# Half-array matmuls of a hybrid attention and state space trunk, run on the whole array

## Chip, cores and metric

One core of a Trainium2 chip runs the whole program; the other cores are idle. The metric is the device time of one execution in microseconds, as the median of several runs, without what the host does.

## What is computed

Two layers of a trunk on 512 tokens of width 1024. Each layer normalises and modulates its input, mixes tokens in three branches (differential attention, latent attention, a gated state space branch), merges them through gates, and ends with a gated feed-forward block with a short convolution. The parts that the change touches, cut down:

```
# differential attention: 4 heads, two maps m of 64 features each
s = einsum('bhqmd,bhkmd->mbhqk', q, k) * 64**-0.5 + bias, causal
p = softmax(s);  out = einsum('bhqk,bhkv->bhqv', p[0] - lam * p[1], v)
# latent attention: 8 heads, 96 features for scores, 64 for values
p = softmax(einsum('bhqd,bhkd->bhqk', q, k) * 96**-0.5, causal)
out = einsum('bhqk,bhkd->bhqd', p, v)
# state space: 16 heads, chunks of 128 tokens
cs = cumsum(dt * a);  decay = exp(cs[l] - cs[s]), causal within a chunk
```

Inputs, weights and result are fp32.

## The kernel before

Tokens or features lie on the 128 partitions, and nearly all work is products on TensorE. Most of them take operands split in a high and a low part, both in the faster fp32r format: `mm3` (L141 to L143) issues high times high, high times low and low times high into one PSUM bank. Weights come by DMA in pieces of 512 KB, ScalarE makes the high part (L132), VectorE the low part (L133). `feat_groups` (512 tokens as moving columns) and `tok_groups` (L220 to L222, 256 columns) yield after every few products, so that they can be laid between others. Some products are plain fp32, which the trace records twice each.

A planner orders all engines' work by its own estimates, and picks the engine where the code says `nc.any`. In the two attentions TensorE's order is written out by hand instead (`manual_schedule`): `run` issues a unit's scores, some filling products (`fill`, from the gates, branches and next projections), an earlier unit's transposes, more filling, and the weighted values of one still earlier.

PSUM has two pools: "mb" for the large products, "ab" for the rest, five banks in the attentions.

- State space branch (`mix`, a group of four heads at a time). `decays` leaves the sums of the steps' logarithms in `cs_r`, 48 rows: 16 heads' high parts in rows 0 to 15, their low parts in rows 32 to 47. For each head a product of `sel`'s column with `cs_r` (L953) spreads one head's row over 128 partitions; VectorE makes `dec` from it (L955).
- Latent attention. Units are a head and a tile of 128 queries; heads are taken in pairs whose values lie side by side in `vv`, 64 columns each. `mla_unit`'s scores are an `mm3` on 96 rows, its softmax ends at L1156, `weights_T` transposes the probabilities (L1136), and `values` (L1168) multiplies 64 columns of `vv` by them. The two heads of a pair write the two halves of one bank, which is copied to `o_feat` when both are done (L1171). The scores run two units ahead of the transposes and three ahead of the values.
- Differential attention. `da_transpose` leaves for each map a tile of queries (high parts in the map's own 64 rows, low parts in the other 64) and one of keys (high parts in both), so that one product on 128 rows gives high times high and low times high (L1292). Queries' high parts times keys' low parts are a second product on the map's own 64 rows (L1293), with the keys' low parts of both maps in one tile `kl`. A unit has two such pairs of products, one for each map, with max(256, 128 (t + 1)) columns for the tile t of queries.

Of the kernel before, what the change touches and what calls it, by code (L numbers as in the profile page):

```python
# [9 lines left out]
F32 = mybir.dt.float32  # L10
# [8 lines left out]
P = 128  # L19
S = 512  # L20
# [45 lines left out]
def trunk_kernel(ctx: ExitStack, tc: tile.TileContext, a: dict, out: bass.AP):  # L66
# [26 lines left out]
    # ---------------------------------------------------------------- constants  # L93
# [9 lines left out]
    sel = cst.tile([48, SSM_H], F32R, name="sel")  # L103
    nc.vector.tensor_copy(out=sel[0:32], in_=ident[0:32, 0:SSM_H])
# [8 lines left out]
    # ---------------------------------------------------------------- weights  # L113
# [42 lines left out]
    def feat_groups(w, cols, nk, rhs, evac):  # L156
        """Two tiles of 128 output features; w is [nk*128, n], cols their first columns.
        A group is a function that fetches weights and one that yields after some products."""
        st = {}
        joined = cols[1] == cols[0] + P  # L160

        def group(k0):
            n = min(4, nk - k0)

            def prep():
                rows = w[k0 * P:(k0 + n) * P, :].rearrange("(k p) c -> p k c", p=P)
                if joined:
                    raw = load([(0, (n, 256), rows[:, :, cols[0]:cols[0] + 256])])
                    view = "p (k i c) -> p i k c"
                else:  # L170
                    raw = load([(i * n * P, (n, P), rows[:, :, c:c + P]) for i, c in enumerate(cols)])
                    view = "p (i k c) -> p i k c"
                wh, wl = split(raw, n * 256)
                bg(2)
                return [x[:, 0:n * 256].rearrange(view, k=n, i=2) for x in (wh, wl)]

            def mm(weights):
                vh, vl = weights
                if k0 == 0:
                    st["banks"] = [mbank(), mbank()]  # L180
                for k in range(n):
                    xh, xl = rhs(k0 + k)
                    for i in range(2):
                        mm3(st["banks"][i], vh[:, i, k], vl[:, i, k], xh, xl, k0 + k == 0, k0 + k == nk - 1)
                    if k0 + k == nk - 1:
                        for i in range(2):
                            evac(i, st["banks"][i])
                    yield 1.28
            return prep, mm
        return [group(k0) for k0 in range(0, nk, 4)]  # L190

    def tok_groups(w, segs, hh, hl, evac):
        """Up to 256 output columns, tokens on partitions."""
# [37 lines left out]
    def feat_halves(w, cols, nk, rhs, evac, joint, pool=None, spare=0):  # L231
        """As feat_groups, the tokens' first half before the second. With joint, evac gets whole rows.
        The weights of the last groups, spare in number, go to a pool of their own."""
# [35 lines left out]
    def latent_product(l, pool, hh, hl):  # L269
        """Tokens' latent queries, latent keys and values, rotary key and step sizes, a half of the tokens after the other.  # L270
        The weights of the last group go to a pool of their own."""
# [43 lines left out]
    def seam(last, norm, first, us):  # L315
        """The last two products before a norm and the first one after it, in halves of the tokens."""
# [41 lines left out]
    # ---------------------------------------------------------------- small vectors of a layer  # L358
# [3 lines left out]
    def mod_vectors(l, vp):  # L362
        """Bias of the modulation, the norms' gains, the state space branch's taps."""
# [69 lines left out]
    # ---------------------------------------------------------------- rotary tables  # L433
# [31 lines left out]
    # ---------------------------------------------------------------- conditioning  # L465
# [25 lines left out]
    # ---------------------------------------------------------------- modulation  # L491
    mod = [cst.tile([P, 48], F32, name=f"mod{l}") for l in range(DEPTH)]

    def mod_steps(l, j, pool=None):
        """Steps that together give 512 columns of a layer's modulation."""
# [46 lines left out]
    def mod_steps_pe(l, j, pool):  # L542
        """The same with products on the tensor engine."""
# [20 lines left out]
    def mod_queue(l, chunks):  # L564
        """Steps of several chunks; a chunk's sums over partitions come within the next chunk."""
        out, late = [], None
        for j in chunks:
            todo = mod_steps(l, j)
            out += todo[0:4] + ([late] if late else []) + todo[4:-1]
            late = todo[-1]  # L570
        return out + [late]

    # ---------------------------------------------------------------- relative bias, in blocks of causal tiles
# [10 lines left out]
    def rel_tables(bp):  # L584
        """Key positions, queries' positions less the buckets' starts, block-diagonal table of steps."""
# [8 lines left out]
        # differences of neighbouring buckets; halves of them, and of the ends' sum, for steps of -1 and 1  # L594
# [40 lines left out]
    def rel_bias(bp, tables, t, g):  # L635
        """Bias of 32 queries of a tile for all heads; a column of four queries needs the keys up to them only."""
# [31 lines left out]
    # ---------------------------------------------------------------- modulated norm  # L668
    def norm_r(np_, x_tok):
        """A token's reciprocal root mean square, on all partitions; after a step for each tile of tokens."""  # L670
# [33 lines left out]
    def norm_halves(np_, x, l, v_norm, sh0, sc0):  # L704
        """The norm of tiles whose last four come in halves of the tokens, as steps for seam()."""
# [35 lines left out]
    # ---------------------------------------------------------------- token mixing  # L741
    def mix(l, x, hh, hl, ckr, cq, latp, scope):
        """Gated sum of the branches, twice over."""
# [49 lines left out]
        # ---- latents of the latent attention  # L793
# [47 lines left out]
        cs_r = ssd.tile([48, S], F32R, name="cs_r")  # L841
        nc.vector.tensor_copy(out=cs_r, in_=zeros[0:48])
        cs, ncs, tot, ecs, te = (ssd.tile([P, T, SSM_H], F32, name=nm) for nm in ("cs", "ncs", "tot", "ecs", "te"))

        def decays():
            """Sums of the steps' logarithms within chunks, and what follows from them."""
# [17 lines left out]
        # ---- state space branch, a group of four heads at a time  # L864
        ys = []
        with ssd_scope:
            tails = []
            for g in range(SSM_G):
# [81 lines left out]
                for r in range(4):  # L950
                    h = 4 * g + r
                    lp_ = abank()
                    nc.tensor.matmul(lp_, sel[:, h:h + 1].broadcast_to([48, P]), cs_r, start=True, stop=True)  # L953
# [47 lines left out]
        with ExitStack() as att:  # L1001
# [6 lines left out]
            def feed(groups):  # L1008
                """Queues products that fill the gaps; the weights of the first two are fetched at once."""
                todo.extend(groups)  # L1010
                while len(ahead) < min(2, len(todo)):
                    ahead.append(todo[len(ahead)][0]())
# [11 lines left out]
            def fill(us=None):  # L1024
                """Filling products for about that many microseconds, or all that is queued."""
                owed[0] = owed[0] + us if us else 1e9
                while owed[0] > 0.6:
                    cost = next(filling)
                    owed[0] = owed[0] - cost if cost else 0.0
# [14 lines left out]
            # ---- latent attention, two heads at a time  # L1044
            def rope(x, n, cc, ss_, o):
                """x, o: [P, n.., 32]; cc, ss_ tables of the same shape"""
# [94 lines left out]
            def mla_unit(pr, h, t):  # L1141
# [20 lines left out]
                def values():  # L1162
                    if t == 0 and h == 0:
                        pairs[pr]["o"] = abank()
                    po, vv = pairs[pr]["o"], pairs[pr]["v"]
                    own = slice(h * MLA_V, (h + 1) * MLA_V)
                    for j in range(t + 1):
                        nc.tensor.matmul(po[own, t * P:n], vv[:, j, own], st["pT"][:, j * P:(j + 1) * P],  # L1168
                                         start=j == 0, stop=j == t)
                    if t == T - 1 and h == 1:  # L1170
                        nc.any.tensor_copy(out=o_feat[pr], in_=po)  # L1171
                return scores, turn, values

            def run(units, events, amounts, lag, later={}):
                """Scores of a unit, transposes of an earlier one, weighted values of one still earlier."""
# [51 lines left out]
            # ---- differential attention  # L1227
            ya = []
            heads = [{} for _ in range(DA_H)]

# [23 lines left out]
            def da_transpose(h, i):  # L1254
                """Queries' high parts over low parts, keys' high parts twice, keys' low parts; a tile for each map."""
# [7 lines left out]
                maps = (slice(0, DA_D), slice(DA_D, P))  # L1263
                if i == 1:
                    heads[h]["kl"] = kl = dap.tile([P, S], F32R, name="kl")
                for m, own in enumerate(maps):
# [3 lines left out]
                    lo = o[other] if i == 0 else kl[own]  # L1270
# [5 lines left out]
            def da_unit(h, t):  # L1276
# [3 lines left out]
                def scores():  # L1280
# [6 lines left out]
                    for m in range(2):  # L1287
                        mr = slice(m * DA_D, (m + 1) * DA_D)
# [4 lines left out]
                        nc.tensor.matmul(s_ps[:, 0:w], qT[mr], hd["kl"][mr, 0:w], start=False, stop=True)  # L1293
# [70 lines left out]
    def out_products(l, mo, m_, extra):  # L1364
        """Output projection and residual: the residual, the products of one half, those of the other."""
# [24 lines left out]
    # ---------------------------------------------------------------- gated conv feed-forward  # L1390
    class Ffn:
        """Blocks of features go through the up projection, the conv, the gate and the down projection."""
# [27 lines left out]
        def run(self, fp, extra):  # L1420
            """All but the last two products, which are returned."""
# [28 lines left out]
    # ---------------------------------------------------------------- the end  # L1450
    def finish(last, x):
        """The last product in halves of the tokens, whose rows go out as they come."""
# [30 lines left out]
    # ---------------------------------------------------------------- the trunk  # L1483
# [93 lines left out]
```

## Time and profile before

| | |
|---|---|
| median of 3 runs | 2136.69 us (2134.92 to 2140.43) |
| span of the profiled execution | 2134.3 us |
| TensorE products busy | 2109.5 us, 99% |
| TensorE weight loads busy | 1785.0 us, 84% |
| VectorE busy | 1416.2 us, 66% |
| ScalarE busy | 918.8 us, 43% |
| granted TensorE clock, mean | 0.999 |

The profile is of one execution. Its span runs from the first instruction to the last; the page gives no other time of that execution, and the median of the runs lies 2.4 us above the span. A product's end is modelled and overlaps the next one's start, so for TensorE the distance between starts tells the pace. "PE" is a product, "PEld" the load of its stationary operand; "128*64 128x128" is 128 rows by 64 columns of the array and a moving operand of 128 rows and 128 columns. An fp32 product stands as two records.

### The profile page before, as it was taken

Reading aid. Unit: us, or ns where it says so; the run is one execution under the profiler, and the core shown is the slowest. Engines: PE = TensorE matmul, PEld = TensorE weight load, DVE = VectorE, ACT = ScalarE, POOL = GpSimd, SP = SyncE. Lnnn points to the kernel's source line nnn. Section 1 sums busy time; section 2 is a strip of 40 time slices with the busy share of each in tenths; the row PEclk is TensorE's granted clock in tenths of the full one; section 3 lists DMA queues with packets and bytes.
Section 4 is the critical chain, followed back from the end, with each engine's and each line's share of the span. In section 5 each row is a group of like instructions: output and inputs, shape, how many; then the busy total and the mean of one; then the engine's idle time right before and its main releaser. Section 6 shows DMA issues by size and latency. Waiting matters only on the chain.

```text
span 2134.3 us, 30137 instructions
## 1 busy us (share of the span) xinstructions
PE 2109.5 (99%) x11469; PEld 1785.0 (84%) x11469; DVE 1416.2 (66%) x2730; ACT 918.8 (43%) x1689; POOL 137.5 (6%) x162
## 2 busy tenths in 40 slices
PE   7999999999999999999999999999999999999999
PEld 7888887788878988888898888878897888888888
DVE  7888877646766678658767787764566456553563
ACT  6644445434443354223344444454444334432441
POOL 4200011001100000000000000110110000000000
PEclk9999999999999999999999999999999999999999
DMA  7522242233444355555433222112232233323322
GB/s 264 148 75 79 65 131 81 71 112 98 149 137 148 113 179 169 190 177 164 154 128 95 64 70 82 56 47 73 86 88 83 87 129 99 96 93 98 99 87 82
DMA packets 224541, 237.19 MB, mean 111 GB/s; under 512 B 16126, under 2 KB 195742, under 8 KB 224142
## 3 DMA queue, kind: packets, MB, share of 16 engines
q1 hardware_dynamic: 221646, 232.63, 35.0%
q0 software_dynamic: 2752, 2.65, 0.5%
q8 instruction: 90, 1.47, 0.3%
q14 instruction: 53, 0.43, 0.1%
HBM read 226.30 MB, written 8.91 MB: 110 GB/s over the span
## 4 chain that ended last, share of the span: by engine, by line
PE 85%; DVE 5%; issue 5%; DMA 2%; POOL 1%; ACT 0%; SPq 0%; POOLq 0%; DVEq 0%; ACTq 0%
PE mb L141 20%; PE mb L142 20%; PE mb L143 20%; PE mb L220 3%; PE mb L222 3%; PE mb L221 3%; PE ab L1168 2%; PE ab L1136 1%; PE ab L1293 1%; DVE macc L518 1%; DMA wg<-in_ada_w_dram 1%; PE ab L961 1%; PE ab L1315 1%; PE ab L1292 1%; DVE wl L133 1%
## 5 line engine op out<-in xcount | busy, mean ns | idle before, releaser
L141 PE MATMUL mb<-hh,wh 128*128 128x512 f32 (+1 forms) x1376 | 541.2, 394 | 1.8 <-DVE modsum L530 0.9
L142 PE MATMUL mb<-hl,wh 128*128 128x512 f32 (+1 forms) x1376 | 533.0, 387 | 0.0
L143 PE MATMUL mb<-hh,wl 128*128 128x512 f32 (+1 forms) x1376 | 532.6, 387 | 0.0
L133 DVE TENSOR_TENSOR wl<-wr,wh 128x1024 fp32r<-128x1024 f32 (+2 forms) x312 | 374.9, 1203 | 211.9 <-ACT wh L132 209.5
L132 ACT ACTIVATE wh<-wr 128x1024 fp32r<-128x1024 f32 (+2 forms) x312 | 324.4, 1041 | 353.2 <-PE mb L142 270.8
L141 PEld LDWEIGHTS mb<-hh,wh 128*128 128x128 f32 x1376 | 258.4, 188 | 58.7 <-issue 6.4
L143 PEld LDWEIGHTS mb<-hh,wl 128*128 128x128 f32 x1376 | 258.6, 188 | 51.0
L142 PEld LDWEIGHTS mb<-hl,wh 128*128 128x128 f32 x1376 | 258.9, 188 | 50.0 <-issue 2.0
L1412 DVE SCALAR_TENSOR_TENSOR fu<-mb,vec,fu 128x510 f32<-128x510 f32 (+1 forms) x176 | 129.9, 746 | 92.0 <-ACT fu L1410 90.5
L220 PE MATMUL mb<-wh,hh 128*128 128x256 f32 x640 | 183.8, 287 | 0.0
L221 PE MATMUL mb<-wl,hh 128*128 128x256 f32 x640 | 181.0, 283 | 0.0
L222 PE MATMUL mb<-wh,hl 128*128 128x256 f32 x640 | 181.0, 283 | 0.0
L141 PE MATMUL mb<-gh,wh 128*128 128x512 f32 (+1 forms) x432 | 152.2, 352 | 0.0
L143 PE MATMUL mb<-gh,wl 128*128 128x512 f32 (+1 forms) x432 | 151.5, 351 | 0.0
L142 PE MATMUL mb<-gl,wh 128*128 128x512 f32 (+1 forms) x432 | 151.5, 351 | 0.0
L1410 ACT ACTIVATE fu<-mb,vec 128x512 f32<-128x512 f32 x88 | 67.7, 772 | 149.7 <-PE mb L143 149.7
L220 PEld LDWEIGHTS mb<-wh,hh 128*128 128x128 f32 x640 | 122.5, 191 | 3.1 <-issue 0.7
L221 PEld LDWEIGHTS mb<-wl,hh 128*128 128x128 f32 x640 | 122.6, 192 | 0.4
L222 PEld LDWEIGHTS mb<-wh,hl 128*128 128x128 f32 x640 | 122.6, 192 | 0.0
L518 DVE SCALAR_TENSOR_TENSOR macc<-wg,c_act,macc 128x512 f32<-128x512 f32 x140 | 104.8, 748 | 19.9 <-DMA wg<-in_ada_w_dram 19.1
L141 PE MATMUL mb<-yh,wh 128*128 128x512 f32 x256 | 105.8, 413 | 0.0
L142 PE MATMUL mb<-yl,wh 128*128 128x512 f32 x256 | 101.1, 395 | 0.0
(333 smaller groups left out, 3416.3 us busy)
## 6 DMA issues: line engine op xcount, KB each, us to landing
wr<-in_w_in_dram SPq DMA_DIRECT2D x88, 512.0 KB
wr<-in_ffn_w_up_dram SPq DMA_DIRECT2D x88, 512.0 KB
wg<-in_ada_w_dram SPq DMA_DIRECT2D x160, 256.0 KB
wr<-in_ffn_w_down_dram SPq DMA_DIRECT2D x40, 512.0 KB
wr<-in_w_in_dram SPq DMA_DIRECT2D x64, 256.0 KB
wm<-in_ada_w_dram SPq DMA_DIRECT2D x16, 512.0 KB
wr<-in_w_branch_c_dram SPq DMA_DIRECT2D x16, 512.0 KB
wr<-in_w_out_dram SPq DMA_DIRECT2D x16, 512.0 KB
```

The costliest lines, as they stand in the source:

```text
L132: nc.scalar.activation(hi[:, sl], raw[:, sl], AF.Copy)
L133: nc.vector.tensor_tensor(out=lo[:, sl], in0=raw[:, sl], in1=hi[:, sl], op=ALU.subtract)
L141: nc.tensor.matmul(o, lh, rh, start=first, stop=False)
L142: nc.tensor.matmul(o, lh, rl, start=False, stop=False)
L143: nc.tensor.matmul(o, ll, rh, start=False, stop=last)
L220: nc.tensor.matmul(o, hh[:, kk, ts_], wh[:, sl], start=first and k == 0, stop=False)
L221: nc.tensor.matmul(o, hh[:, kk, ts_], wl[:, sl], start=False, stop=False)
L222: nc.tensor.matmul(o, hl[:, kk, ts_], wh[:, sl], start=False, stop=last and k == 3)
L518: ins = nc.vector.scalar_tensor_tensor(out=acc[0], in0=rk, scalar=c_act[:, kk:kk + 1], in1=acc[0], op0=ALU.mult, op1=ALU.add)
L1168: nc.tensor.matmul(po[own, t * P:n], vv[:, j, own], st["pT"][:, j * P:(j + 1) * P], start=j == 0, stop=j == t)
L1410: nc.scalar.activation(u, bank, AF.Identity, bias=v[:, V_FCB + ti:V_FCB + ti + 1], scale=tap(2))
L1412: nc.vector.scalar_tensor_tensor(out=u[:, s_:], in0=bank[:, 0:S - s_], scalar=tap(2 - s_), in1=u[:, s_:], op0=ALU.mult, op1=ALU.add)
```

## The change

All three products get operands for the whole array.

- The state space sums: `sel` and `cs_r` grow from 48 to 128 rows, the rest zero.
- The latent attention's values: the product takes both heads' 128 columns of `vv`. Each head has its own bank, and the 64 partitions that belong to the head are copied when its four tiles are done.
- The differential attention's low parts: in place of `kl` there are two tiles, `kl0` and `kl1`, one for each map, with the other map's 64 rows cleared once a layer. The second product takes all 128 rows of queries and of that tile.

Comments and some texts of functions are also taken out, which moves no line.

```
-    sel = cst.tile([48, SSM_H], F32R, name="sel")
-    nc.vector.tensor_copy(out=sel[0:32], in_=ident[0:32, 0:SSM_H])
+    sel = cst.tile([P, SSM_H], F32R, name="sel")
+    nc.vector.tensor_copy(out=sel, in_=ident[:, 0:SSM_H])
     nc.vector.tensor_copy(out=sel[32:48], in_=ident[0:SSM_H, 0:SSM_H])
...
-        cs_r = ssd.tile([48, S], F32R, name="cs_r")
-        nc.vector.tensor_copy(out=cs_r, in_=zeros[0:48])
+        cs_r = ssd.tile([P, S], F32R, name="cs_r")
+        nc.vector.tensor_copy(out=cs_r, in_=zeros)
...
-                    nc.tensor.matmul(lp_, sel[:, h:h + 1].broadcast_to([48, P]), cs_r, start=True, stop=True)
+                    nc.tensor.matmul(lp_, sel[:, h:h + 1].broadcast_to([P, P]), cs_r, start=True, stop=True)
...
-                    if t == 0 and h == 0:
+                    if t == 0:
                         pairs[pr]["o"] = abank()
                     po, vv = pairs[pr]["o"], pairs[pr]["v"]
                     own = slice(h * MLA_V, (h + 1) * MLA_V)
                     for j in range(t + 1):
-                        nc.tensor.matmul(po[own, t * P:n], vv[:, j, own], st["pT"][:, j * P:(j + 1) * P],
+                        nc.tensor.matmul(po[:, t * P:n], vv[:, j], st["pT"][:, j * P:(j + 1) * P],
                                          start=j == 0, stop=j == t)
-                    if t == T - 1 and h == 1:
-                        nc.any.tensor_copy(out=o_feat[pr], in_=po)
+                    if t == T - 1:
+                        nc.any.tensor_copy(out=o_feat[pr][own], in_=po[own])
...
+            maps = (slice(0, DA_D), slice(DA_D, P))
+            blank = dap.tile([P, S], F32, name="sb", bufs=4)
+            nc.vector.memset(blank, 0.0)
+            kls = []
+            for m in range(2):
+                kls.append(dap.tile([P, S], F32R, name=f"kl{m}"))
+                nc.vector.tensor_copy(out=kls[m][maps[1 - m]], in_=blank[maps[1 - m]])
...
-                maps = (slice(0, DA_D), slice(DA_D, P))
-                if i == 1:
-                    heads[h]["kl"] = kl = dap.tile([P, S], F32R, name="kl")
                 for m, own in enumerate(maps):
...
-                    lo = o[other] if i == 0 else kl[own]
+                    lo = o[other] if i == 0 else kls[m][own]
...
-                        mr = slice(m * DA_D, (m + 1) * DA_D)
...
-                        nc.tensor.matmul(s_ps[:, 0:w], qT[mr], hd["kl"][mr, 0:w], start=False, stop=True)
+                        nc.tensor.matmul(s_ps[:, 0:w], qT, kls[m][:, 0:w], start=False, stop=True)
```

## Rows read from the trace of the kernel before

**Rows 1.** The page: busy time, share of the span and instructions of each engine.

```profile
PE 2109.5 (99%) x11469; PEld 1785.0 (84%) x11469; DVE 1416.2 (66%) x2730; ACT 918.8 (43%) x1689; POOL 137.5 (6%) x162
```

**Rows 2.** The page: the chain that ended last, share of the span by engine.

```profile
PE 85%; DVE 5%; issue 5%; DMA 2%; POOL 1%; ACT 0%; SPq 0%; POOLq 0%; DVEq 0%; ACTq 0%
```

**Rows 3.** Windows of layer 0: the state space branch, the latent attention with what follows it, the differential attention. Columns: stretch, its length, busy time (and instructions) of PE, PEld, DVE, ACT and POOL, granted clock, DMA share, GB/s.

```profile
125.00:310.00 185.00, 183.72 (x1059) 157.49 (x1058) 150.43 (x271) 85.82 (x183) 9.98 (x9) 1.00 0.28 81
310.00:470.00 160.00, 158.46 (x941) 130.39 (x940) 102.64 (x281) 74.19 (x159) 17.60 (x17) 1.00 0.29 89
470.00:640.00 170.00, 169.95 (x977) 142.70 (x976) 117.49 (x253) 74.96 (x147) 21.74 (x23) 1.00 0.41 128
```

**Rows 4.** The products of L1168, L1293 and L953, one answer each: count, duration in ns (least, median, most), first and last start, shapes with their counts.

```profile
L1168 PE MATMUL ab<-pT,vv x320: 272/273/324, 321.3 to 1471.5; 128*64 128x128 f32 x160
...
L1293 PE MATMUL ab<-kl,qk x64: 377/410/498, 474.5 to 1651.6; 64*128 64x256 f32 x32, 64*128 64x384 f32 x16, 64*128 64x512 f32 x16
...
L953 PE MATMUL ab<-cs_r,sel x32: 383/491/498, 130.3 to 1308.2; 48*128 48x512 f32 x32
```

**Rows 5.** Timeline of TensorE's products around a unit of the differential attention with 256 columns: start in us, duration in us, line, names, shape.

```profile
473.82 0.39 PE L142 MATMUL mb<-hl,wh 128*128 128x512 f32 x1
474.05 0.39 PE L143 MATMUL mb<-hh,wl 128*128 128x512 f32 x1
474.28 0.28 PE L1292 MATMUL ab<-qk,qk 128*128 128x256 f32 x1
474.49 0.38 PE L1293 MATMUL ab<-kl,qk 64*128 64x256 f32 x1
474.80 0.38 PE L1292 MATMUL ab<-qk,qk 128*128 128x256 f32 x1
...
475.42 0.38 PE L220 MATMUL mb<-wh,hh 128*128 128x256 f32 x1
475.64 0.28 PE L221 MATMUL mb<-wl,hh 128*128 128x256 f32 x1
475.76 0.28 PE L222 MATMUL mb<-wh,hl 128*128 128x256 f32 x1
```

**Rows 6.** The weight loads of the same stretch; in brackets idle time ahead of a load and what ended it.

```profile
473.83 0.19 PEld L143 LDWEIGHTS mb<-hh,wl 128*128 128x128 f32 x1
...
474.49 0.18 PEld L1293 LDWEIGHTS ab<-kl,qk 64*128 64x128 f32 x1 [0.24 <-issue]
```

**Rows 7.** Timeline of TensorE's products: ends of a unit of the differential attention with 384 columns and of one with 512 (between them stand L1292, L1293, L1292, L1293 and a large product), and two 384-column products on 96 rows in the latent attention.

```profile
492.94 0.38 PE L1315 MATMUL ab<-tok,pT 128*128 128x128 f32 x2
...
494.88 0.40 PE L142 MATMUL mb<-hl,wh 128*128 128x512 f32 x1
...
501.95 0.39 PE L1315 MATMUL ab<-tok,pT 128*128 128x128 f32 x2
...
504.12 0.39 PE L142 MATMUL mb<-yl,wh 128*128 128x512 f32 x1
...
329.56 0.34 PE L142 MATMUL ab<-knl,qnh 96*128 96x384 f32 x1
329.74 0.34 PE L143 MATMUL ab<-knh,qnl 96*128 96x384 f32 x1
```

**Rows 8.** Timeline of TensorE's products in the latent attention: a run of four value records followed by scores, a run of eight followed by four transposes and scores, and the first run of the next head.

```profile
324.81 0.40 PE L143 MATMUL mb<-yh,wl 128*128 128x512 f32 x1
...
325.94 0.28 PE L142 MATMUL ab<-knl,qnh 96*128 96x256 f32 x1
...
331.20 0.39 PE L143 MATMUL mb<-yh,wl 128*128 128x512 f32 x1
331.52 1.09 PE L1168 MATMUL ab<-pT,vv 128*64 128x128 f32 x8
...
333.25 0.40 PE L142 MATMUL ab<-knl,qnh 96*128 96x512 f32 x1
...
335.43 0.43 PE L1168 MATMUL ab<-pT,vv 128*64 128x128 f32 x2
```

**Rows 9.** The values of the differential attention, L1315: a run of six records and the product behind it in the timeline, and, from the weight loads grouped by line and shape, those of L1168 and of L1315 (busy us, mean ns, idle before).

```profile
513.56 0.83 PE L1315 MATMUL ab<-tok,pT 128*128 128x128 f32 x6
514.14 0.36 PE L1292 MATMUL ab<-qk,qk 128*128 128x256 f32 x1
...
L1168 PEld LDWEIGHTS ab<-pT,vv 128*64 128x64 f32 x320 | 33.2, 136 | 19.0 <-issue 13.1 <-ACT sb L1154 4.7 <-DVE sums L1155 0.4
...
L1315 PEld LDWEIGHTS ab<-tok,pT 128*128 128x128 f32 x160 | 22.1, 191 | 1.8
```

**Rows 10.** Timeline of TensorE's products around one of the state space sums: the product ahead of it and the second one behind it.

```profile
136.82 0.39 PE L143 MATMUL mb<-hh,wl 128*128 128x512 f32 x1
...
137.90 0.40 PE L142 MATMUL mb<-hl,wh 128*128 128x512 f32 x1
```

**Rows 11.** TensorE's waits for split weights, whole span: who waited for what, us in total, times, longest.

```profile
PE mb L295 <- ACT wh L132: 1.4, 1, 1.4
```

**Rows 12.** The copies of the latent attention's values by VectorE; one softmax's last step on VectorE and the weight load of the transposes that read it, from the timelines.

```profile
L1171 DVE COPY o_feat<-ab x6: 680/680/692, 349.3 to 1471.8; 128x512 f32<-128x512 f32 x6
...
328.61 0.29 DVE L1156 TENSOR_SCALAR sb<-sb,sums 128x128 f32<-128x128 f32 x1
...
329.74 0.14 PEld L1136 LDWEIGHTS ab<-ident,sb 128*128 128x128 f32 x1
```

## The prediction

> **What bounds the kernel now.** I read the page's busy times and clock first, then the chain of waits, then busy time by stage, then single lines of TensorE, last TensorE's timeline around the products that the change touches.
>
> TensorE is busy for 2109.5 of 2134.3 us [rows 1]. The windows give a granted clock of 1.00, which is the 2.4 GHz level [rows 3], so no time is to be had from the clock. The chain that ended last is 85% TensorE, 5% "issue" and 5% VectorE [rows 2]. In the state space stage, the latent attention and the differential attention TensorE is busy 183.7 of 185, 158.5 of 160 and 169.95 of 170 us, while VectorE has 151, 103 and 117 us there and ScalarE less [rows 3]. A nanosecond taken off TensorE's stream should therefore be a nanosecond off the run, as long as VectorE keeps up.
>
> "Busy" says nothing about pace, though, because ends of products are modelled and overlap. Pace is the distance from one start to the next. Full-array products with 512 columns start 0.23 us apart, with 256 columns 0.12 [rows 5]. On 96 rows the 384-column step is 0.18, in line with these two [rows 7]. The fp32 products of the differential attention's values, all 128 rows and columns, take 0.11 each: six records between 513.56 and 514.14, the last of them only 0.03 ahead of its successor, a shift that I saw at every change from fp32 to the split format and that the next product pays back [rows 9].
>
> Now the products of the change. The low-part product on 64 rows starts 0.21 us after its full-array neighbour, the next one 0.31 after that, and the second product behind the pair still 0.22 after the first, all with 256 columns where 0.12 is the pace [rows 5]. The reason is in the weight loads: an ordinary load starts while the product before it runs (L143's at 473.83 against L142's product at 473.82), but the 64-row one starts only with its own product, 474.49 [rows 6]. Weights aren't fetched ahead into or out of a half array. The same appears at the 64-column values and at the 48-row sums, while 96 rows run at full pace [rows 7, 8, 10]. So it is the small shapes (64 and fewer) that stall, on entering and on leaving.
>
> **The change, part by part.** I cost each as the stretch from the product before the small ones to the second one behind, less what the full-array pace gives.
>
> *Differential attention, low parts.* 64 products in 32 units, two to a unit, each between full products: 16 units with 256 columns, 8 with 384, 8 with 512 [rows 4].
> 256: 474.28 to 475.64 is 1.36, five products at 0.12 are 0.60, the excess is 0.76 [rows 5].
> 384: 492.94 to 494.88 is 1.94; 2 x 0.11 + 4 x 0.18 + 0.23 = 1.17; excess 0.77. 512: 501.95 to 504.12 is 2.17; 2 x 0.11 + 5 x 0.23 = 1.37; excess 0.80 [rows 7].
> Sum 16 x 0.76 + 8 x 0.77 + 8 x 0.80 = 24.7 us. Afterwards these are full-array products on zero rows, as wide as before; columns set the pace, so they cost the 0.12 to 0.23 already in the sum.
>
> *Latent attention, values.* 320 records [rows 4], in 62 unbroken runs (one per unit of 64, two pairs of units follow each other directly). Followed by scores: 324.81 to 325.94 is 1.13; 0.23 + 4 x 0.11 + 0.12 = 0.79; excess 0.34. Followed by transposes: 331.20 to 333.25 is 2.05; L143, eight values, four transposes and one 512-column product give 0.23 + 12 x 0.11 + 0.23 = 1.78; excess 0.27 [rows 8]. Both kinds are common, so I take 0.305: 18.9 us.
> The new form, 64 more columns of weights in this place, isn't in the trace. Its bounds: the pace stays 0.11, as for L1315, which loads 128x128 fp32 in 191 ns and yet steps at 0.11; or the load is exposed and the step becomes 0.19 [rows 9]. L1315 has the same formats and sizes, so I take 0.11. At 0.19 the loss would be 320 x 0.08 = 26 us.
> Here a rule speaks against the change. The Trainium skill ("TensorE: Matmul & The Clock Gate", Part 2, LDWEIGHTS) has a load's time grow with its columns, whatever its rows: at its 1.2 columns per ns 64 more columns would be 53 ns, 17 us for 320 loads if none is hidden, which would leave 36 us of gain. The trace has the growth (136 against 191 ns in the loads' rows) but hides it at L1315 [rows 9].
>
> *State space sums.* 32 products on 48 rows [rows 4], in 24 runs (each group of four heads makes two single ones and one pair). 136.82 to 137.90 is 1.08 against 3 x 0.23 = 0.69: 0.39 a run [rows 10], 9.4 us together.
>
> *What is added.* Per layer a clear of one 128x512 tile and two 64x512 copies to the zero halves, and one more copy of a values bank for each of four pairs: seven instructions, each at most the 0.68 us of the present 128x512 copy [rows 12], so at most 4.8 us of VectorE per layer. VectorE idles 57 us in the 310 to 470 window [rows 3], which hides them. If that cover were gone, the clear and the copies stand ahead of the first keys' low part and could hold the first scores 3 x 0.68 = 2 us per layer. The key rows' copies per head are as many as before, only into other tiles; no DMA is moved.
>
> *What is late next.* Weights' splits: TensorE now waits 1.4 us for them in the whole run [rows 11]. Softmax: the shortest lead I found is early in the latent attention, probabilities scaled by 328.90, their transposes' load at 329.74, 0.84 us to spare [rows 12]. That unit spans two or three runs of values, so it arrives 0.6 to 0.9 us earlier; at worst it waits 0.1 us. Four such units per layer: I give back 1 us at most.
>
> Sum: 24.7 + 18.9 + 9.4 = 53.0 us less 1 = 52. The profiled span is 2134.3 and would be about 2082; the median of the runs, 2136.7, lies 2.4 above the span, so 2136.7 - 52 = 2085 us.
>
> **The rivals.**
> *Feeders become the bound.* With TensorE some 3 to 7% shorter in these stages, VectorE (81% of the state space window now [rows 3]) and the softmax chains could return half of what those two stages gain: (18.9 + 9.4) / 2 = 14, 2099 us. For it: VectorE's share, and the planner may order the state space stage anew. Against: TensorE idles 1.3 us there now, so nothing was late.
> *The wider load is exposed* (26 us above): 2085 + 26 = 2111 us. Against it stands L1315.
> *The change doesn't do what it says:* the gaps belong to something else, such as accumulating in one bank with swapped operands, and stay: 2137, no change. Against it: three lines with nothing in common but the small shape show them, and 96-row products that accumulate alike don't [rows 7]. A mechanism with the same outcome: full-height loads are never fetched ahead, so filling the array only exchanges one exposed load for another. The Trainium skill says this nearly ("TensorE: Matmul & The Clock Gate", Part 3, The mechanism: loads overlap products in flight only where the row groups differ). By that rule, no gain; the trace differs, with L143's full-height load beginning 0.01 us after L142's product [rows 5, 6].
> *Slower: the values' bank.* Each head now takes a PSUM bank of its own from a pool of five, 16 hand-overs instead of 8, in an order of TensorE that is written out. The next head's first values come at 335.43, after the last values of the head before that began at 331.5 [rows 8] and end eight records later, near 332.5; the copy takes 0.68 [rows 12], so the bank has some 2.2 us to spare. If copies queued up behind splits, TensorE would stand still at each hand-over. To end more than 0.3% (6.4 us) slower, the 16 waits must eat 52 + 6.4, 3.7 us each, that is, copies must come 5.9 us late. At 4 us each: 2085 + 64 = 2149 us. Nothing in the waits points there.
>
> **How the numbers follow.** Forecast as summed: 0.77. Feeders: 0.11. Exposed load: 0.03. No change: 0.05. Bank: 0.03. The last 0.01 goes to an order so lucky that it beats the sum. The prediction is the likeliest, 2085. Its own spread: the per-run excesses are good to 0.03 us over 32 + 62 + 24 runs, 3.5 us, and the planner's new order some us more, so 2077 to 2093. For eight in ten the range reaches on to the feeders' case, 2077 to 2103; it leaves out the exposed load, the unchanged and the slower case, about one in ten. About 0.3% is what a measurement of this kernel can tell from no change. Faster: 0.77 + 0.11 + 0.03 + 0.01 = 0.92; same 0.05; slower 0.03.
>
> **What would show it.** Right: the low-part products read 128*128 and start 0.12 to 0.23 us after their neighbours; their loads begin during the product before; the values' runs step at 0.11 with 128 columns; "issue" ahead of the values' loads, 13.1 us now [rows 9], is nearly gone; a layer's latent attention is some 9 us shorter, the differential one 12, the state space stage 5. Wrong: the same starts 0.2 to 0.3 apart at 128*128 (no change), steps near 0.19 in the values (exposed load), VectorE or ScalarE as releaser ahead of L1136 or the split weights (feeders), or a wait at a head's first values (bank).

## The result and the profile after

The changed kernel takes 2089.55 us at the median (2087.19 to 2092.36), the kernel before 2135.95 beside it; the ratio is 0.9776, with a 95% interval of 0.9763 to 0.9788, so 2.2% faster. Timed a second time it took 2087.02 against 2137.32, 0.9765 (0.975 to 0.9779). The forecast was 2085, with a range of 2077 to 2103. The profiled execution has a span of 2085.2 us and itself took 2087.19, the shortest of the first four.

A unit of the differential attention with 256 columns after the change, TensorE's products in the timeline, to be held against [rows 5]. L1296 and L1297 are the former L1292 and L1293.

```profile
462.03 0.39 PE L143 MATMUL mb<-hh,wl 128*128 128x512 f32 x1
462.26 0.28 PE L1296 MATMUL ab<-qk,qk 128*128 128x256 f32 x1
462.38 0.28 PE L1297 MATMUL ab<-kl,qk 128*128 128x256 f32 x1
462.49 0.28 PE L1296 MATMUL ab<-qk,qk 128*128 128x256 f32 x1
462.61 0.28 PE L1297 MATMUL ab<-kl,qk 128*128 128x256 f32 x1
462.73 0.28 PE L220 MATMUL mb<-wh,hh 128*128 128x256 f32 x1
462.85 0.28 PE L221 MATMUL mb<-wl,hh 128*128 128x256 f32 x1
```

The weight loads of the same stretch, as in [rows 6]:

```profile
462.04 0.19 PEld L1296 LDWEIGHTS ab<-qk,qk 128*128 128x128 f32 x1
462.26 0.19 PEld L1297 LDWEIGHTS ab<-kl,qk 128*128 128x128 f32 x1
```

The same five products that took 1.36 us from the first L1292 to the second one behind the pairs take 0.59, from 462.26 to 462.85. L1297's load starts with the product before it, at 462.26, and no longer with its own.

A run of the latent attention's values followed by scores, in TensorE's timeline, as the first one of [rows 8]:

```profile
321.55 0.40 PE L143 MATMUL mb<-yh,wl 128*128 128x512 f32 x1
321.79 0.61 PE L1168 MATMUL ab<-pT,vv 128*128 128x128 f32 x4
322.15 0.36 PE L141 MATMUL ab<-knh,qnh 96*128 96x256 f32 x1
322.35 0.28 PE L142 MATMUL ab<-knl,qnh 96*128 96x256 f32 x1
```

The weight loads of both attentions' values, grouped by line and shape (count, busy us, mean ns, idle before), as in [rows 9]:

```profile
L1168 PEld LDWEIGHTS ab<-pT,vv 128*128 128x128 f32 x320 | 43.8, 191 | 3.9
L1319 PEld LDWEIGHTS ab<-tok,pT 128*128 128x128 f32 x160 | 22.1, 191 | 1.8
```

From L143 to the second product of the scores it is now 0.80 us instead of 1.13. The loads grew from 136 to 191 ns, and the "issue" ahead of them, 13.1 us before, is no longer named.

One of the state space sums in TensorE's timeline, as in [rows 10]:

```profile
137.37 0.39 PE L143 MATMUL mb<-hh,wl 128*128 128x512 f32 x1
137.59 0.39 PE L953 MATMUL ab<-cs_r,sel 128*128 128x512 f32 x1
...
138.05 0.39 PE L142 MATMUL mb<-hl,wh 128*128 128x512 f32 x1
```

From L143 to the second product behind the sum it is 0.68 us instead of 1.08.

Where the time went, by stage: windows of the state space branch, the latent attention and the differential attention, three for each layer, cut at the same instructions in both kernels. First the kernel before, then the one after; columns as in [rows 3].

```profile
112.20:293.40 181.20, 180.34 (x1082) 156.53 (x1082) 145.83 (x250) 83.64 (x181) 5.38 (x5) 1.00 0.27 77
293.40:455.20 161.80, 161.19 (x938) 132.07 (x937) 108.21 (x304) 74.15 (x163) 21.34 (x22) 1.00 0.29 90
455.20:639.80 184.60, 183.19 (x1062) 154.58 (x1061) 125.48 (x263) 82.18 (x157) 22.60 (x24) 1.00 0.42 130
1148.00:1329.20 181.20, 180.34 (x1082) 156.54 (x1082) 144.08 (x247) 83.65 (x181) 5.36 (x5) 1.00 0.26 72
1329.20:1489.10 159.90, 159.90 (x930) 131.19 (x929) 95.09 (x280) 73.85 (x162) 20.30 (x22) 1.00 0.20 58
1489.10:1671.20 182.10, 181.72 (x1049) 153.27 (x1048) 105.74 (x226) 82.23 (x157) 21.75 (x23) 1.00 0.29 86
```

```profile
113.40:290.10 176.70, 175.84 (x1082) 157.23 (x1081) 145.94 (x250) 83.65 (x180) 5.33 (x5) 1.00 0.28 79
290.10:443.20 153.10, 152.13 (x938) 135.56 (x937) 108.53 (x306) 76.07 (x168) 21.96 (x22) 1.00 0.32 95
443.20:617.00 173.80, 170.81 (x1061) 152.35 (x1060) 125.26 (x263) 81.44 (x157) 21.64 (x24) 1.00 0.45 138
1125.30:1302.10 176.80, 175.95 (x1083) 157.25 (x1082) 144.24 (x247) 83.73 (x181) 5.37 (x5) 1.00 0.26 74
1302.10:1452.50 150.40, 150.40 (x929) 134.61 (x928) 94.64 (x279) 77.47 (x170) 20.29 (x22) 1.00 0.22 61
1452.50:1622.20 169.70, 169.32 (x1050) 151.30 (x1049) 105.44 (x226) 81.45 (x157) 20.10 (x23) 1.00 0.32 92
```

The second column gives the gains: state space 4.5 and 4.4 us, latent attention 8.7 and 9.5, differential attention 10.8 and 12.4, together 50.3. In these windows the number of products is the same within one and the granted clock is 1.00 in both. The start up to the first window is 1.2 us longer, which makes the spans' difference of 49.1. That is not the change's doing as far as the profiles show: the first product of L853, which comes just ahead of the first window in all kernels, starts at 111.2 us before and 112.5 after, and between 110.1 and 117.0 in the eleven profiles of this document. The granted clock up to there was 0.94 after and 0.98 before; the differential part's kernel below, at 1.00, still started at 112.7, so the clock alone doesn't explain it. The differential attention of layer 0 gains less than that of layer 1, and TensorE is idle there for 3.0 us where it was 1.4. TensorE's waits in that window name what is new; the first line is the only one of the same window before, the others are those after:

```profile
PE ab L1261 <- DVE qkn L1243: 1.4, 1, 1.4
```

```profile
PE ab L1269 <- DVE qkn L1251: 1.4, 1, 1.4
PE mb L141 <- ACT g L765: 0.9, 1, 0.9
PE mb L141 <- DVE g L774: 0.7, 1, 0.7
```

The gates' banks come free too late twice, for 1.6 us in all, which is the difference between the two layers.

### The profile page after: what moved, and what is told of

Same layout as the page of the kernel before. It is cut to its first block, busy times and chain, and to the rows that moved or that the text cites. A ratio compares the mean times of both kernels' runs of the same rounds, so it can differ in the third digit from the quotient of the medians.

```text
span 2085.2 us, 30158 instructions
## 1 busy us (share of the span) xinstructions
PE 2060.7 (99%) x11469; PEld 1794.4 (86%) x11469; DVE 1415.1 (68%) x2731; ACT 923.4 (44%) x1702; POOL 136.0 (7%) x162
## 4 chain that ended last, share of the span: by engine, by line
PE 85%; DVE 5%; issue 5%; DMA 2%; POOL 1%; ACT 1%; SPq 0%; POOLq 0%; DVEq 0%; ACTq 0%
PE mb L141 20%; PE mb L142 20%; PE mb L143 20%; PE mb L220 3%; PE mb L222 3%; PE mb L221 3%; PE ab L1168 2%; PE mb L662 1%; PE ab L1136 1%; DMA wg<-in_ada_w_dram 1%; DVE wl L133 1%; PE ab L961 1%; DVE macc L518 1%; PE ab L1319 1%; PE ab L1078 1%
## 5 line engine op out<-in xcount | busy, mean ns | idle before, releaser
L141 PE MATMUL mb<-hh,wh 128*128 128x512 f32 (+1 forms) x1376 | 538.5, 392 | 2.9 <-DVE modsum L530 1.4
L143 PE MATMUL mb<-hh,wl 128*128 128x512 f32 (+1 forms) x1376 | 532.9, 387 | 0.0
L142 PE MATMUL mb<-hl,wh 128*128 128x512 f32 (+1 forms) x1376 | 532.5, 387 | 0.0
L141 PEld LDWEIGHTS mb<-hh,wh 128*128 128x128 f32 x1376 | 258.6, 188 | 53.4 <-DVE modsum L530 2.6
L143 PEld LDWEIGHTS mb<-hh,wl 128*128 128x128 f32 x1376 | 258.7, 188 | 51.4
L142 PEld LDWEIGHTS mb<-hl,wh 128*128 128x128 f32 x1376 | 259.0, 188 | 49.0 <-DVE hl L698 1.2
L221 PE MATMUL mb<-wl,hh 128*128 128x256 f32 x640 | 181.2, 283 | 0.0
L141 PE MATMUL mb<-gh,wh 128*128 128x512 f32 (+1 forms) x432 | 152.3, 353 | 0.0
L143 PE MATMUL mb<-gh,wl 128*128 128x512 f32 (+1 forms) x432 | 151.7, 351 | 0.0
L142 PE MATMUL mb<-gl,wh 128*128 128x512 f32 (+1 forms) x432 | 151.7, 351 | 0.0
L221 PEld LDWEIGHTS mb<-wl,hh 128*128 128x128 f32 x640 | 122.6, 192 | 0.4
L141 PE MATMUL mb<-yh,wh 128*128 128x512 f32 x256 | 105.4, 412 | 0.9 <-ACT g L765 0.9
L142 PE MATMUL mb<-yl,wh 128*128 128x512 f32 x256 | 101.2, 395 | 0.0
```

What stands on the lines that cost most here:

```text
L141: nc.tensor.matmul(o, lh, rh, start=first, stop=False)
L142: nc.tensor.matmul(o, lh, rl, start=False, stop=False)
L143: nc.tensor.matmul(o, ll, rh, start=False, stop=last)
L221: nc.tensor.matmul(o, hh[:, kk, ts_], wl[:, sl], start=False, stop=False)
```

## The experiments

**One part at a time.** The kernel before with one of the three parts of the diff each.

```
# e1_da: kl0 and kl1 with zero rows, L1293 on 128 rows; the rest as before
# e2_mla: values on 128 columns, a bank for each head; the rest as before
# e3_ssm: sel and cs_r on 128 rows; the rest as before
```

> The differential attention's part alone: full-array low parts on zero rows, the values and the state space sums as before. Theory (products on 64 rows or columns and fewer cost a stall at each way in and out): 24.7 us less than before by the sum, 23 as the whole change's trace has it, so a ratio of 0.988 to 0.9893, and the starts of the low parts 0.12 to 0.23 apart. Rival (the gain came from the planner's new order or from the parts together): this part alone gives under half of it, a ratio over 0.994.

> The latent attention's part alone: values with both heads' 128 columns and a bank for each head. Theory: 18 to 19 us less than before, a ratio of 0.991 to 0.992; the loads take 191 ns instead of 136 and the step stays at 0.11 us. Rival (gain by order or by the parts together): a ratio over 0.9955.

> The state space part alone: sums on 128 rows. Theory: 9 to 9.5 us less than before, a ratio of 0.9955 to 0.996. Rival (the state space stage waits for VectorE and gives the time back): under 4 us, a ratio over 0.998.

Measured beside 2137.07 of the kernel before: the differential part 2111.98 (25.1 us, ratio 0.9886, 0.9871 to 0.99), the latent part 2117.97 (19.1 us, 0.9912, 0.9895 to 0.9928), the state space part 2129.79 (7.3 us, 0.9962, 0.9947 to 0.9977). Each part carries its own gain, near its excess of 24.7, 18.9 and 9.4 us, so the gain isn't a matter of the parts together, nor of a new order in one stage. The state space part alone is the least certain one: 7.3 at the median, under the 9 to 9.5 that were expected, while its interval reaches from 4.9 to 11.3. The three add to 51.5; the whole change gave 46.4 and 50.3. From these times alone it can't be told whether the parts lose a little to each other or only scatter.

The profiles can tell more, since the start, which differs from execution to execution, can be left out: from the first product of L853 to the end of the span. The kernel before and the changed one:

```profile
L853 PE MATMUL ab<-tri,da x16: 272/273/283, 111.2 to 1147.8; 128*16 128x128 f32 x16
L853 PE MATMUL ab<-tri,da x16: 272/272/283, 112.5 to 1125.1; 128*16 128x128 f32 x16
```

So counted, before takes 2134.3 - 111.2 = 2023.1 us, and the changed kernel 50.4 less (50.8 in the profile of its second timing). The differential part saves 22.5, the latent part 19.4 and the state space part 9.8, 51.7 together. The parts nearly add, and the state space part's gain is not low there. These are single executions, though; the two of the changed kernel differ by 0.4.

**Half products side by side.** The kernel before, with both full products of a unit ahead of both 64-row ones.

```
+                    sps = [abank() for _ in range(2)]
+                    for m in range(2):
+                        nc.tensor.matmul(sps[m][:, 0:w], hd[0, m][:, t * P:n], hd[1, m][:, 0:w], start=True, stop=False)
                     for m in range(2):
                         mr = slice(m * DA_D, (m + 1) * DA_D)
...
-                        nc.tensor.matmul(s_ps[:, 0:w], qT, kT, start=True, stop=False)
-                        nc.tensor.matmul(s_ps[:, 0:w], qT[mr], hd["kl"][mr, 0:w], start=False, stop=True)
+                        nc.tensor.matmul(sps[m][:, 0:w], hd[0, m][mr, t * P:n], hd["kl"][mr, 0:w], start=False, stop=True)
```

> The kernel before with the four products of a differential unit in another order: both full ones, then both on 64 rows (two ways in and out of a half array instead of four). Theory (the stall belongs to the switch, some 0.19 us each): 32 units save two switches, 12 us, less up to 0.1 us a unit if the second half product's load is not fetched ahead either: 9 to 12 us, a ratio of 0.9945 to 0.996. If the two half products also overlap, since they use different rows, up to 17 us, 0.992. Rival (the stall belongs to each small product, wherever it stands): no change, 0.999 to 1.001.

2120.25 us, 16.8 less than before, ratio 0.9921 (0.9907 to 0.9936): the case with overlap. The timeline of TensorE's products in the first unit (L1290 full, L1293 on 64 rows):

```profile
474.29 0.39 PE L1290 MATMUL ab<-qk,qk 128*128 128x256 f32 x2
474.61 0.38 PE L1293 MATMUL ab<-kl,qk 64*128 64x256 f32 x2
474.93 0.39 PE L220 MATMUL mb<-wh,hh 128*128 128x256 f32 x1
475.15 0.28 PE L221 MATMUL mb<-wl,hh 128*128 128x256 f32 x1
```

Two products on 64 rows stand in one row of 0.38 us, and the next product starts 0.32 us after them, where one alone took 0.31 [rows 5]: they run at once, on different rows of the array. From the first L1290 to L221 it is 0.86 us, against 1.36 before [rows 5] and 0.59 on the whole array: two switches of 0.19 and one product of 0.12 less than before. So the stall belongs to the switch between half and whole array, not to each small product. Even so the pair loses to two whole products: at these widths (0.12 to 0.23 a product) what overlap saves doesn't pay for two switches of 0.19.

**Neither half nor whole.** The kernel before with the sums on 72 rows, and the values on 96 columns: each head's own 64 and 32 of the other's. Each head again has its own bank, and its 64 partitions are copied in two pieces of 32.

```
-    sel = cst.tile([48, SSM_H], F32R, name="sel")
+    sel = cst.tile([72, SSM_H], F32R, name="sel")
...
-                        nc.tensor.matmul(po[own, t * P:n], vv[:, j, own], st["pT"][:, j * P:(j + 1) * P],
+                        nc.tensor.matmul(po[0:96, t * P:n], vv[:, j, 32 * h:32 * h + 96], st["pT"][:, j * P:(j + 1) * P],
```

> The kernel before with the state space sums on 72 rows and the latent attention's values on 96 columns (each head its own 64 and 32 of the other's), neither on the whole array; the differential attention as before. Theory (the stall belongs to shapes of 64 and fewer): the same gain as these two parts on the whole array had, 19 + 7 to 9.5 = 26 to 28.5 us, a ratio of 0.9865 to 0.988, sums 0.23 from the product before and values 0.11 apart with no gap around them. Rival (only the whole array is free of the stall): no change, or half of it if one of rows and columns behaves so.

2111.9 us beside 2137.32, 25.4 less, ratio 0.988 (0.9863 to 0.9896): the same as the two whole-array parts, 19.1 + 7.3 = 26.4, within the intervals. The start in its profile is the longest of the eleven (117.0); without the start it saves 28.0, beside 19.4 + 9.8 = 29.2. TensorE's timeline at a run of values and at a pair of sums:

```profile
326.22 0.39 PE L143 MATMUL mb<-yh,wl 128*128 128x512 f32 x1
326.45 0.60 PE L1168 MATMUL ab<-pT,vv 128*96 128x128 f32 x4
326.80 0.36 PE L141 MATMUL ab<-knh,qnh 96*128 96x256 f32 x1
327.00 0.28 PE L142 MATMUL ab<-knl,qnh 96*128 96x256 f32 x1
...
140.00 0.39 PE L961 MATMUL ab<-xdt,dec 128*128 128x64 f32 x2
140.19 0.71 PE L953 MATMUL ab<-cs_r,sel 72*128 72x512 f32 x2
140.75 0.40 PE L141 MATMUL mb<-hh,wh 128*128 128x512 f32 x1
140.98 0.39 PE L142 MATMUL mb<-hl,wh 128*128 128x512 f32 x1
```

From L143 to the second product of the scores 0.78 us, as on the whole array (0.80), and L142 follows L141 at 0.23 behind the sums. So only shapes that fit in half of the array stall: 48 and 64 rows and 64 columns do, 72 rows, 96 rows and 96 columns don't. Rows between 64 and 72 and columns between 64 and 96 weren't tried. The Trainium skill ("TensorEngine Tiling (Array Packing)", Key Properties) says that changing the tiling mode drains TensorE, and its Available Configurations list rows of 128, 64 and 32; of these 72 rows fit only the 128. The trace agrees in that 72 rows run without a stall, where each switch to or from 64 rows cost 0.19 us.

**Overlapping column halves.** If halves overlap, long runs of them should beat the whole array. The changed kernel, with the two heads of a pair taking turns and the values of both issued together as 64-column products. The same edit moves two of the next pair's transposes by a unit and goes back to one bank and one copy for a pair.

```
-                units += [mla_unit(pr, h, t) for h in range(2) for t in range(T)]
+                units += [mla_unit(pr, h, t) for t in range(T) for h in range(2)]
...
+                        for g in range(2):
+                            own = slice(g * MLA_V, (g + 1) * MLA_V)
+                            nc.tensor.matmul(po[own, t * P:n], vv[:, j, own], pairs[pr]["pT", g][:, j * P:(j + 1) * P],
+                                             start=j == 0, stop=j == t)
```

> The changed kernel with the latent attention in another order: the two heads of a pair take turns, tile by tile, and the values of both are issued together as 64-column products in turn on the two column halves, in one bank. Theory: the halves run at the same time as the two row halves did in the pairs run, so a tile's values take half the slots: (t + 1) x 4 records of 0.11 become half, 0.55 us saved a pair of units on average, less one way in and out, 0.3: 0.25 x 32 = 8 us less than the changed kernel, a ratio to before of 0.973 to 0.975. Rival (fp32's two passes don't overlap across column halves): the values cost as before and each pair of units adds a stall, 32 x 0.3 = 10 us more than the changed kernel, 0.982. A third case: the new order of units makes scores wait for transposes, any time over 0.978.

> The changed kernel itself again, beside the others on one chip: 0.977 to 0.979 by its first comparison. The three parts alone saved 25.1, 19.1 and 7.3 us, 51.5 together; if the parts simply add, 0.976, if together they meet new waits, 0.978.

2086.01 us, ratio 0.9762 (0.9747 to 0.9776), beside 2087.02 of the changed kernel itself, 0.9765: no difference, where 8 us were expected. (The changed kernel's own 0.9765 lies between the 0.976 and 0.978 that its expectation set apart, nearer to parts that simply add.) The products do overlap. The values of two heads for tile 3 in TensorE's timeline:

```profile
343.85 1.09 PE L1172 MATMUL ab<-pT,vv 128*64 128x128 f32 x16
344.88 0.48 PE L1100 MATMUL ab<-wm,lat 128*128 128x256 f32 x1
```

Sixteen records take 1.09 us, as long as eight took before [rows 8]. But the new order brings transposes and values too close behind the softmax. TensorE's waits in this kernel, whole span:

```profile
PE ab L1136 <- DVE sb L1156: 2.6, 5, 0.8
PE ab L1172 <- DVE pT L1138: 1.2, 2, 0.6
```

The windows of the two latent attentions, columns as in [rows 3], show where the gain went:

```profile
289.40:442.50 153.10, 149.79 (x938) 124.87 (x937) 108.90 (x307) 72.95 (x163) 21.77 (x22) 1.00 0.31 95
1301.00:1450.50 149.50, 147.87 (x929) 124.20 (x929) 95.10 (x282) 72.97 (x163) 21.24 (x22) 1.00 0.21 62
```

TensorE is busy 2.3 and 2.5 us less than in the changed kernel (152.13 and 150.40) but idle for 3.3 and 1.6 us, where it was idle for 1.0 and 0.0. The stages are as long as in the changed kernel or 0.9 us shorter. So of the 8 us that were expected 4.9 show as less busy time; the two waits above, 3.8 us, take most of that back, and why the other 3 didn't come stays open.

**Dealing the filling out anew.** Two attempts to take these waits away, in the column halves kernel. The four numbers belong to the tiles 0 to 3; that of tile 1 stays. (The column halves run has these waits three times in layer 0 and twice in layer 1, the longest 0.8 us for the product; the expectation below put them higher.)

```
-MLA_SHAPE = (1.2, 0.8, 0.95, 1.1)
+MLA_SHAPE = (0.8, 0.8, 1.15, 1.25)
# e9_fill, besides:
-MLA_FILL = (1.36, 1.38, 1.44, 1.76, 2.66)
+MLA_FILL = (1.8, 1.6, 1.6, 1.76, 1.6)
```

> As the column halves run, with the filling products of a unit dealt out anew: fewer beside tiles 0 and 1, more beside tiles 2 and 3 (0.8, 0.8, 1.15, 1.25 for 1.2, 0.8, 0.95, 1.1), where transposes waited 0.7 to 1.2 us for the softmax in the column halves run, three times a layer. Theory (what the overlapping values saved went into those waits): 3 to 5 us less than the column halves run, a ratio to before of 0.974 to 0.975. Rival (the waits only move): 0.976 as there.

> The same, and the filling products also moved towards the first pairs of heads (1.8, 1.6, 1.6, 1.76, 1.6 for 1.36, 1.38, 1.44, 1.76, 2.66). Theory: the first pair's waits, the longest, go too: 4 to 6 us less than the column halves run, 0.9735 to 0.9745. Rival: too few are left for the last pair, whose values wait then: 0.976 or more.

2085.33 us, ratio 0.9757 (0.9743 to 0.977), and 2092.73, 0.9801 (0.9788 to 0.9815), both beside 2136.55. By its time the first isn't told apart from the column halves run or from the changed kernel. Without the start its one profile is 2.4 us shorter than the column halves run's and 3.3 shorter than the changed kernel's second one, and no product of the transposes waits for L1156 any more; a single execution of each is thin for such a difference. The second is slower than both. The largest wait of TensorE in the second, whole span:

```profile
PE mb L141 <- ACT g L765: 6.1, 3, 3.0
```

And the place of the longest in layer 1, in TensorE's timeline, with the window behind it:

```profile
1372.53 0.80 PE L141 MATMUL mb<-yh,wh 128*128 128x512 f32 x1 [2.10 <-ACT g L765]
```

```profile
1372.50:1375.00 2.50, 2.47 (x6) 1.99 (x7) 1.53 (x3) 1.42 (x2) 0.00 (x0) 0.50 0.02 7
```

With the filling dealt out so, the gates' banks come free late. Such a wait costs more than its length: behind it the granted clock is 0.50, the 1.2 GHz level, and six products take 2.5 us, 0.42 each, where products of 512 columns start 0.23 apart at the 2.4 GHz level [rows 5]. The longest wait, 2.96 us in layer 0, is followed by the same. So in the second the waits moved, from the softmax to the gates; neither version's time beats the changed kernel's by more than a measurement can tell.

## Why the prediction was right

- *TensorE's stream is the bound, and time off it is time off the run:* held. The windows shortened by 50.3 us; 52 were forecast for the run, 46.4 and 50.3 were measured, and the rest of the run is as long as it was but for the start.
- *The stall belongs to shapes of 64 and fewer, on the way in and out:* held, by the run with 72 rows and 96 columns and by the pairs run. That weights aren't fetched ahead there fits the sizes as well, as the last section shows.
- *The terms:* 24.7, 18.9 and 9.4 were forecast; the windows show 23.2, 18.2 and 8.9, the single parts 25.1, 19.1 and 7.3 by their times and 22.5, 19.4 and 9.8 without the start. The first of the windows' figures lacks the 1.6 us at the gates. The state space term was a little too large: all 24 runs were priced as the single sum, which saved 0.40 us, while the eight pairs saved 0.33 each (median distance before and after), which makes 9.0.
- *The wider load stays hidden:* held. The load takes 191 ns, the values still step at about 0.11. The 26 us of the rival did not come; the growth of the load itself did, by 55 ns.
- *Full-height loads are fetched ahead:* held, L1297's load starts with the product before it, though both fill all rows.
- *What is added:* no wait of TensorE shows for it, as forecast, but the work went elsewhere: all 16 copies of the values' banks went to ScalarE (L1171, 580 ns each), none to VectorE.
- *What is late next:* mis-sized and misplaced. I gave back 1 us to the softmax in the early latent attention, where L1136 waits 0.5 us after and 0.2 before; 1.6 us came back in the differential attention of layer 0, at the gates' banks, which I hadn't looked at. The differential part alone has that wait too (2.1 us for L765 and L774), so it doesn't take the three together.
- *The 4.6 us between 2085 and 2089.55:* the span was forecast at 2082.3 and is 2085.2; 1.7 of these 2.9 us are in the windows and 1.2 in the start, which no run ties to the change. The rest is scatter: the profiled execution took 2087.19, the other three up to 2092.36, and the second timing has a median of 2087.02.
- *The bank for each head:* no wait shows at a head's first values, as forecast.

## What to carry to other kernels

Where a stream of full-array products is the bound, look at the distance between starts around every product with 64 or fewer rows or columns: each switch between a half array and the whole one cost 0.13 to 0.20 us here, about a product's own time, and zero rows or another head's columns removed it without making a product longer. Half products can pay only where running two at once saves more than two switches cost, and no run here beat the whole array by them. Once TensorE is ahead, look for the next late release of a bank before counting on more.

## What the runs showed of the hardware that wasn't expected

Two products on different 64-row halves, or on different 64-column halves, ran at the same time: two 64-row products with 256 columns in 0.32 us to the next product, where one alone took 0.31, and sixteen 64-column fp32 records in the 1.09 us of eight. The Trainium skill says so ("TensorE: Matmul & The Clock Gate", Part 3, The mechanism), and the trace agrees. The prediction had not counted on it, and the expectation of the pairs run only as its further case; it holds for fp32 products, which stand as two records each, too.

What a switch costs is about the duration of the weight load that isn't fetched ahead. Two 64-row products lost 1.36 - 0.59 = 0.77 us, and the loads in and out take 2 x (0.18 + 0.19) = 0.74. A single 48-row sum lost 1.08 - 0.68 = 0.40, with loads of 0.18 and 0.19. A run of 64-column values lost 1.13 - 0.80 = 0.33 ahead of scores, with loads of 0.136 and 0.19, but only 0.27 by the prediction's working ahead of the transposes of L1119, whose load is shorter, 0.126:

```profile
L1119 PEld LDWEIGHTS ab<-ident,kn 128*96 128x96 f32 x64 | 6.5, 126 | 2.7 <-issue 1.7 <-DVE kn L1112 0.7 <-DVE qnl L1124 0.3
```

So the 0.34 and 0.27 that the prediction averaged are two cases with a reason. The sizes agree; no run was made to test this alone.
